# Routing a two-block transformer layer's tokens to 16 experts: selection on logits, facts of the slots in single-pass float32r, idle products in other places, another order of the last rows

## The chip, the cores and the metric

The kernel runs on one core of a Trainium2 chip. The metric is the device time of one execution in microseconds (us); where several executions were timed, their median is given.

## The reference

256 tokens of 1024 features, batch 1, float32, go through two blocks of one layer each. The first block is attention over one key block, retention and a gated feed-forward. The second block has a gated delta rule, a sparse attention over selected keys, a merge of both by two gates, a residual, and then the mixture of experts, which is what this document is about: four groups of four experts; every token takes its best group, in it its two best experts, and weighs them by the probability of the group times the two experts' probabilities, normalized to one. Behind it stands one last normalization of each token.

```python
def hier_moe(h, w_rg, b_rg, w_re, b_re, w1, w3, w2):
    xt = h.reshape(-1, d)                              # h = rmsnorm_2(x, norm2_g)
    glog = (xt @ w_rg + b_rg).astype(jnp.float32)
    gp = jax.nn.softmax(glog, axis=-1)
    gsel = jnp.argmax(glog, axis=-1)
    ggate = jnp.take_along_axis(gp, gsel[:, None], axis=-1)
    elog = (xt @ w_re + b_re).astype(jnp.float32).reshape(-1, N_GROUPS, EXPERTS_PER_GROUP)
    elog_g = jnp.take_along_axis(elog, gsel[:, None, None], axis=1)[:, 0]
    ep = jax.nn.softmax(elog_g, axis=-1)
    top_p, top_i = lax.top_k(ep, TOPK_IN_GROUP)
    top_p = top_p / jnp.sum(top_p, axis=-1, keepdims=True)
    wts = ggate * top_p
    eid = gsel[:, None] * EXPERTS_PER_GROUP + top_i
    comb = jnp.sum(jax.nn.one_hot(eid, N_EXPERTS) * wts[..., None], axis=1)
    act = jax.nn.silu(jnp.einsum("nd,edf->nef", xt, w1)) * jnp.einsum("nd,edf->nef", xt, w3)
    act = act * comb[:, :, None]
    return jnp.einsum("nef,efd->nd", act, w2).reshape(bsz, s, d)
...
        x = x + hier_moe(...)
    return rmsnorm_2(x, final_norm_g)
```

## The kernel before

**Tiles and weights.** Tokens lie in two halves of 128 (`h` is 0 or 1), features in eight blocks of 128 (`m`). All weights come as 134 chunks of 128 x 2048 floats (1 MB), issued on SP's queue by one function (L341; the last four of every 15 chunks of the experts come as two halves of 512 KB into other buffers); the last 48 chunks are the 16 experts'. An expert has three chunks, two for gate and up (`D_EXPERT` is 256) and one for down. Up to the experts every weight is split into a rounded float32r part and a remainder (`whi`, `wlo`, L357 and L358), and each product is done in three single-pass products; the experts' chunks are used as they are, in two passes of float32. For the experts' weights there is room for 15 chunks; each further chunk waits until products have freed a buffer.

**Order.** A scheduler orders each engine's instructions by their dependences and a modelled time. `issue_after(x)` in the code fixes that an instruction comes behind `x` on its engine. `mm` (L374) is the helper of all products, so nearly all of them have that line. `keep_warm(n, ...)` (L1654) issues `n` products of 128 x 128 by 128 x 256 whose result nobody reads: the idle products.

**Routing (`moe_route`, L1698).** The blocks 6 and 7 of the residual `x` come last. Their squares are summed on TensorE, their part of the 20 router logits is added, `rsqrt` gives the normalization, L1716 makes the logits `lg`. `first_max` (L1687) marks the first maximum of four values: a maximum, two comparisons `e`, a maximum `f`, a comparison. It is called for the group (`oh`, L1696). TensorE then transposes the last two pairs of blocks (`turn_t(2)`, `turn_t(3)`, L1665, eight transposes) and makes 14 idle products. On VectorE (DVE) follow `by` (L1727), `eg` (L1729, the four logits of the chosen group's experts), their maximum `em` (L1730), `ex` (L1732, and the exponential on ScalarE (ACT), L1733), `first_max` twice on the exponentials (`oh1`, then `rest`, `oh2`), `sel`, and `oe` (L1741): 16 marks for each token, two of them set. Two products with a triangle of ones (`slt`) and two more for the groups rank the tokens in each expert (`re`) and group (`rg`, both L1751), behind them stand four idle products. `places` (L1758) compares the ranks with 64 slots: `Se` (L1761) says which token lies in which slot of which expert. `turn_s` (L1668) takes each transposed pair of blocks from PSUM: ACT copies it to `xr` (L1673) and rounds it to `thi` (L1674), GpSimd (POOL) makes the remainder `tlo` (L1675); the second call also stores `xr` to DRAM (`xd`, L1677).

**Experts (`moe`, L1766).** 32 products (eight blocks, two halves, `thi` and `tlo`) with `Se[0]` gather the tokens of the first group's four experts into the slots, and ACT and DVE copy them out as `X[0]` and `X[1]` (L1791, L1789). Two experts of 64 slots each make a pair, and there are eight pairs. Beside this the weights of the tokens are made (`dg`, `gs`, `den`, `we`), and `meta` holds 20 numbers of a token: its number, a one, its normalization, its rank in the group, and 16 weights. POOL makes `Sg` (L1823), the slots of the groups. `pc`, four products (L1834 on), counts the tokens of experts and groups. `facts` (L1840) brings `meta` into the slots: 16 products with `Se` (`pair_facts`, `mtp`) and eight with `Sg` (`group_facts`, `mtg`), in two passes each; DVE copies the result (L1849) and makes the row indices (L1851). By these, POOL's gathers fetch the rows of the pairs 2 to 7 from `xd` (`prow`) and the rows of the groups (`grow`).

For the pair `n` come `gate_up` (16 products in two passes each), `act` (silu on ACT, L1913, a product on DVE, L1915), `turn` (two transposes), `down` (eight products; each half of the result is split into `yhi`, L401, on ACT, and `ylo`, L402, on DVE) and `gather` (products of `E` with `yhi` and `ylo` that add both pairs of a group into `y`). In the loop, `pair_facts` and `group_facts` stand behind `gate_up(0)` and ahead of `act(0)`.

**The rows of a group (`finish`, L1962).** For each half of 512 columns: add `y` to the row (L1967, DVE), square and sum (L1968, ACT), multiply by the gain `fng` (L1969, DVE); then the sums are added (`ss`, L1970), `rsqrt` (eight small DVE steps, up to L444), and the row is scaled, 400 columns on ACT (L1972) and 624 on DVE (L1973). A scatter on POOL (L1978) stores it. There are four groups; the last one ends the kernel. A branch behind it (L2022) would recompute everything densely if a slot list had run over.

## Time and profile before

| | before |
|---|---|
| time, median of 3 runs (us) | 779.59 (777.94, 779.61, 779.59) |
| the profiled execution (us) | 776.29, its span 774.1 |
| busy: TensorE (PE), DVE, ACT, POOL (us) | 743.4, 517.4, 357.3, 98.0 |
| mean granted clock of TensorE | 0.979 of full speed |
| moved by DMA | 153.00 MB, mean 198 GB/s |

TensorE is busy 96% of the span, but this share is a mean over stages with different limits. In the forty equal slices of the span (19.4 us each), the moved bytes are mostly under 280 GB/s, and 349 to 417 GB/s in the five slices ahead of the last one, where the experts' weights come; the granted clock is shown with nine tenths or more in all but four of them, one of which (eight tenths) is the slice from 639 to 658 us, that of the routing. In the rows below, a row of the timeline begins with its start and its duration in us, then engine, line, operation, output and inputs, shapes and types, and how many instructions the row joins; in square brackets stands the idle time of the engine ahead of it and what ended it. PEld is the loading of weights into TensorE, SPq the issuing of a DMA. PEclk is the granted clock as a share of full speed, where 1.00 is 2.4 GHz and 0.50 is 1.2 GHz.

### The profile page before, as it was taken

How to read it: one execution, taken by the hardware profiler on the slowest of the kernel's cores; microseconds unless marked ns; L12 is line 12 of the kernel's file. 1: busy time of each engine (PE TensorE's matmuls, PEld its weight loads, DVE VectorE, ACT ScalarE, POOL GpSimd, SP SyncE). 2: the span in 40 equal slices, each digit the busy share in tenths (PEclk: the TensorE clock that was granted, in tenths of full speed). 3: DMA queues.
4: the chain of work that ended last, by engine and by line, in shares of the span. 5: the costliest groups of instructions: out<-in, count | busy, mean ns of one | idle time of the engine just before them, and what ended most of it. 6: DMA issues, size and time to landing. Idle time of an engine off the chain costs nothing. (4 is left out here: it accounts for less than half of the span.)

```text
span 774.1 us, 13914 instructions
## 1 busy us (share of the span) xinstructions
PE 743.4 (96%) x5544; PEld 645.6 (83%) x5544; DVE 517.4 (67%) x1087; ACT 357.3 (46%) x647; POOL 98.0 (13%) x113
## 2 busy tenths in 40 slices
PE   8999999999999999999999989899999999999994
PEld 7998889899999999999989877898889996433421
DVE  6667487777677666788777988876748744333433
ACT  7356444755554454566575424345545522121221
POOL 1000000200000000030010163410001342502100
PEclk9999999999999999999999988999999998999997
DMA  8764333455554555544432341333168793999990
GB/s 308 274 231 160 129 110 120 160 202 173 181 202 163 185 197 171 200 172 166 163 111 82 110 142 51 94 138 110 56 237 360 275 318 135 349 414 417 417 396 27
DMA packets 32949, 153.00 MB, mean 198 GB/s; under 512 B 9712, under 2 KB 10736, under 8 KB 17648
## 3 DMA queue, kind: packets, MB, share of 16 engines
q1 hardware_dynamic: 22464, 141.70, 50.7%
q0 software_dynamic: 2016, 6.29, 2.2%
q10 hardware_dynamic: 8400, 4.08, 1.9%
q8 instruction: 45, 0.74, 0.4%
q14 instruction: 24, 0.20, 0.1%
HBM read 149.57 MB, written 3.54 MB: 198 GB/s over the span
## 5 line engine op out<-in xcount | busy, mean ns | idle before, releaser
L358 DVE TENSOR_TENSOR wlo<-raw,whi 128x1024 fp32r<-128x1024 f32 (+1 forms) x173 | 213.2, 1237 | 82.3 <-ACT whi L357 80.7
L357 ACT ACTIVATE whi<-raw 128x1024 fp32r<-128x1024 f32 (+1 forms) x173 | 180.2, 1045 | 154.2 <-PE acc L374 77.0
L374 PE MATMUL acc<-hhi,wlo 128*128 128x256 f32 x344 | 99.3, 289 | 2.2 <-DVE wlo L358 2.2
L374 PE MATMUL acc<-hhi,whi 128*128 128x256 f32 x344 | 100.4, 292 | 0.0
L374 PE MATMUL sm<-hhi,whi 128*128 128x256 f32 x352 | 99.5, 283 | 0.0
L374 PE MATMUL sm<-hlo,whi 128*128 128x256 f32 x352 | 99.3, 282 | 0.0
L374 PE MATMUL sm<-hhi,wlo 128*128 128x256 f32 x352 | 99.0, 281 | 0.0
L374 PE MATMUL acc<-hlo,whi 128*128 128x256 f32 x344 | 98.9, 288 | 0.0
L374 PEld LDWEIGHTS acc<-hhi,wlo 128*128 128x128 f32 x344 | 66.0, 192 | 3.9 <-DVE wlo L358 2.4
L374 PEld LDWEIGHTS acc<-hhi,whi 128*128 128x128 f32 x344 | 66.3, 193 | 1.4 <-issue 0.8
L374 PEld LDWEIGHTS acc<-hlo,whi 128*128 128x128 f32 x344 | 66.0, 192 | 0.8 <-issue 0.3
L374 PEld LDWEIGHTS sm<-hhi,wlo 128*128 128x128 f32 x352 | 66.6, 189 | 0.0
L374 PEld LDWEIGHTS sm<-hlo,whi 128*128 128x128 f32 x352 | 66.3, 188 | 0.0
L374 PEld LDWEIGHTS sm<-hhi,whi 128*128 128x128 f32 x352 | 66.0, 188 | 0.0
L374 PE MATMUL sm<-raw,X 128*64 128x512 f32 x256 | 61.2, 607 | 0.0
L463 POOL TENSOR_TENSOR sqacc<-sqacc,sq 128x256 f32<-128x256 f32 x19 | 16.2, 852 | 335.2 <-ACT sq L462 334.5
L374 PE MATMUL acc<-alo,whi 128*128 128x256 f32 x176 | 49.5, 281 | 0.0
L374 PE MATMUL acc<-ahi,wlo 128*128 128x256 f32 x176 | 49.4, 281 | 0.0
L374 PE MATMUL acc<-ahi,whi 128*128 128x256 f32 x176 | 49.3, 281 | 0.0
L374 PEld LDWEIGHTS sm<-raw,X 128*64 128x64 f32 x256 | 18.2, 139 | 35.3 <-issue 34.2
L374 PE MATMUL acc<-xhi,wlo 128*128 128x256 f32 x160 | 45.7, 286 | 1.3 <-DVE wlo L358 1.3
L374 PE MATMUL acc<-xhi,whi 128*128 128x256 f32 x160 | 46.0, 288 | 0.9 <-ACT whi L357 0.9
(472 smaller groups left out, 1670.1 us busy)
## 6 DMA issues: line engine op xcount, KB each, us to landing
raw<-in_W_dram SPq DMA_DIRECT2D x119, 1024.0 KB, 5.0
raw<-in_W_dram SPq DMA_DIRECT2D x27, 512.0 KB, 12.1
raw<-in_W_dram SPq DMA_DIRECT2D x4, 256.0 KB, 5.0
xd<-xr ACTq DMA_DIRECT2D x2, 512.0 KB, 2.7
dec<-in_con_dram ACTq DMA_DIRECT2D x2, 384.0 KB
conm<-in_con_dram SPq DMA_DIRECT2D x1, 576.0 KB, 7.1
xa<-in_xT_dram SPq DMA_DIRECT2D x2, 256.0 KB, 4.8
xb<-in_xT_dram SPq DMA_DIRECT2D x2, 256.0 KB
```

Of the source, the lines that this page charges most:

```text
L357: nc.scalar.activation(h, r, AF.Copy)
L358: nc.vector.tensor_tensor(l, r, h.bitcast(F32), ALU.subtract)
L374: return self.nc.tensor.matmul(out, a, b, start=start, stop=stop, **kw).ins
L463: (eng or nc.gpsimd).tensor_tensor(acc, acc, sq, ALU.add)
```

## The change

- **Selection.** `first_max` runs on the logits `eg` themselves, and `rest` subtracts a large number at the first mark. `ex` is gone; the exponential of `eg - em` is made in `moe`, times `sel`, summed into `den`.
- **`tlo`.** DVE makes the remainders of the last two pairs of blocks in place of POOL: two 128 x 256 subtractions behind `oe`, two behind the first two `Se`. The first two pairs stay on POOL.
- **Idle products.** In place of 14 behind the transposes and four behind the ranking: three ahead of the last router products, two ahead of each group of four transposes, nine behind, five behind the ranking.
- **Counts.** `pc` is fixed behind the gather's last product.
- **Facts.** `meta` is split into two float32r parts (`mhl`, 40 columns: rounded part and remainder), so each of the 24 products is one pass of 40 columns. ACT copies the remainders' sums out of PSUM and DVE adds the others. `Sg` becomes float32r.
- **Rows.** In `finish`, the two additions come behind the last `ylo` (`F.split`), the first half's product with `fng` behind both additions, and the second half's product with `fng` joins its scaling in one step. ACT scales the first 512 columns, DVE the last 512.

```diff
@@ turn_s
-    def turn_s(self, m2, tp):
+    def turn_s(self, m2, tp, after=None):
...
-            nc.gpsimd.tensor_tensor(lo, x, hi.bitcast(F32), ALU.subtract)
+            with self.tc.issue_after(after) if after else contextlib.nullcontext():
+                (nc.vector if after else nc.gpsimd).tensor_tensor(lo, x, hi.bitcast(F32), ALU.subtract)
@@ moe_route
         with self.tc.issue_after(done):
+            self.keep_warm(3, self.slt[:, 0], self.thi[0][:, 0:256])
             for m in (6, 7):
...
-            tp = [self.turn_t(2), self.turn_t(3)]
-            self.keep_warm(14, self.slt[:, 0], self.thi[0][:, 0:256])
+            tp = []
+            for m2 in (2, 3):
+                self.keep_warm(2, self.slt[:, 0], self.thi[0][:, 0:256])
+                tp.append(self.turn_t(m2))
+            self.keep_warm(9, self.slt[:, 0], self.thi[0][:, 0:256])
...
-        nc.vector.tensor_reduce(em[:, :, 0], eg, axis=AX.X, op=ALU.max)
-        ex = self.ex = self.t("c", (2, 4), name="ex")
-        nc.vector.tensor_tensor(ex, eg, em.to_broadcast([128, 2, 4]), ALU.subtract)
-        nc.scalar.activation(ex, ex, AF.Exp)
...
-        self.first_max(oh1, ex, self.m1)
-        nc.vector.scalar_tensor_tensor(rest, oh1, -2.0, ex, op0=ALU.mult, op1=ALU.add)
-        self.first_max(oh2, rest, self.m2)
+        self.first_max(oh1, eg, em)
+        nc.vector.scalar_tensor_tensor(rest, oh1, -BIG, eg, op0=ALU.mult, op1=ALU.add)
+        self.first_max(oh2, rest, self.t("c", (2, 1), name="m2"))
...
+        self.turn_s(2, tp[0], chosen)
...
-            self.keep_warm(4, self.slt[:, 0], self.thi[0][:, 0:256])
+            self.keep_warm(5, self.slt[:, 0], self.thi[0][:, 0:256])
...
         self.places(0)
-        for i in range(2):
-            self.turn_s(2 + i, tp[i])
+        self.turn_s(3, tp[1], self.placed)
@@ moe
+        we = c3("we")
+        nc.vector.tensor_tensor(we, self.eg, b4(self.em), ALU.subtract)
+        nc.scalar.activation(we, we, AF.Exp)
+        nc.vector.tensor_tensor(we, we, self.sel, ALU.mult)
         den = c3("den", 1)
-        nc.vector.tensor_tensor(den, self.m1, self.m2, ALU.add)
+        nc.vector.tensor_reduce(den[:, :, 0], we, axis=AX.X, op=ALU.add)
...
-        we = c3("we")
-        nc.vector.tensor_tensor(we, self.sel, self.ex, ALU.mult)
...
+        mhl = self.t("t1", (2, 40), F32R, name="mhl")
+        nc.vector.tensor_copy(mhl[:, :, 0:20], meta[:, :, 0:20])
+        nc.vector.tensor_tensor(mhl[:, :, 20:40], meta[:, :, 0:20], mhl[:, :, 0:20].bitcast(F32), ALU.subtract)
...
-                    mm(pm[:, i], s[h].bitcast(F32), meta[:, h, 0:20], i == 0 and h == 0, h == 1, skip_group_check=True)
+                    mm(pm[:, i], s[h], mhl[:, h], i == 0 and h == 0, h == 1, skip_group_check=True)
...
-            nc.vector.tensor_copy(mt, pm)
+            nc.scalar.activation(mt, pm[:, :, 20:40], AF.Copy)
+            nc.vector.tensor_tensor(mt, pm[:, :, 0:20], mt, ALU.add)
@@ finish
             for n, o in enumerate(halves):
-                nc.vector.tensor_tensor(o, y[n], o, ALU.add)
+                with self.tc.issue_after(F.split) if F.split else contextlib.nullcontext():
+                    nc.vector.tensor_tensor(o, y[n], o, ALU.add)
                 nc.scalar.activation(y[n], o, AF.Square, accum_out=ss[:, n:n + 1])
-                nc.vector.tensor_tensor(o, o, fng[:, 512 * n:512 * n + 512], ALU.mult)
+            nc.vector.tensor_tensor(halves[0], halves[0], fng[:, 0:512], ALU.mult)
...
-            nc.scalar.activation(row[:, 624:], row[:, 624:], AF.Copy, scale=rr)
-            nc.vector.tensor_scalar(row[:, 0:624], row[:, 0:624], rr, None, op0=ALU.mult)
+            nc.scalar.activation(halves[0], halves[0], AF.Copy, scale=rr)
+            nc.vector.scalar_tensor_tensor(halves[1], halves[1], rr, fng[:, 512:1024], op0=ALU.mult, op1=ALU.mult)
```

The order of TensorE at the routing, as a piece of the difference (`thi,slt` are the idle products, L1665 the transposes, `ms` the router's weights):

```order
 L374 MATMUL sm<-ones,sq 128x1 x4
+L374 MATMUL acc<-thi,slt 128x256 x3
 L374 MATMUL sm<-ms,x_7206 128x20 x4
-L1665 MATMUL acc<-con,x_7206 128x128 x8
-L374 MATMUL acc<-thi,slt 128x256 x14
+L374 MATMUL acc<-thi,slt 128x256 x2
+L1665 MATMUL acc<-con,x_7206 128x128 x4
+L374 MATMUL acc<-thi,slt 128x256 x2
+L1665 MATMUL acc<-con,x_7206 128x128 x4
+L374 MATMUL acc<-thi,slt 128x256 x9
 L374 MATMUL sm<-oe,slt 128x32
```

The idle products, 14 in a row before, now stand ahead of, between and behind the transposes, with three more ahead of the last router products.

DVE at the end of the routing, in the changed kernel:

```order
+L1743 TENSOR_TENSOR oe<-sel,oh 128x32
+L1677 TENSOR_TENSOR tlo<-xr,thi 128x256 x2
+L1754 SCALAR_TENSOR_TENSOR re<-sm,oe 128x32
+L1754 SCALAR_TENSOR_TENSOR rg<-sm,oh 128x8
+L1763 TENSOR_TENSOR Se<-con,re 128x256 x2
+L1677 TENSOR_TENSOR tlo<-xr,thi 128x256 x2
+L1798 TENSOR_TENSOR dg<-ms,gm 128x8
```

Before, `oe`, `re`, `rg`, the two `Se` and `dg` followed each other directly; two pairs of `tlo` have moved in between.

DVE at the end of the kernel, as a piece of the difference (the rows of the last group, whose last `ylo` is the fourth of the row `x4`):

```order
-L1967 TENSOR_TENSOR row<-acc,row 128x512
-L402 TENSOR_TENSOR ylo<-acc,yhi 128x512
-L1969 TENSOR_TENSOR row<-row,fng 128x512
-L1967 TENSOR_TENSOR row<-acc,row 128x512
-L1969 TENSOR_TENSOR row<-row,fng 128x512
-L1970 TENSOR_TENSOR ss<-ss 128x1
+L1984 SCALAR_TENSOR_TENSOR row<-row,ry,fng 128x512
+L1925 SCALAR_TENSOR_TENSOR ea__8436<-sm,rc,sl 128x256
+L402 TENSOR_TENSOR ylo<-acc,yhi 128x512 x4
+L1978 TENSOR_TENSOR row<-acc,row 128x512 x2
+L1980 TENSOR_TENSOR row<-row,fng 128x512
+L1981 TENSOR_TENSOR ss<-ss 128x1
```

The last `ylo` now stands ahead of both additions, and one product with `fng` is gone from between them and the sum.

## Rows read from the trace of the kernel before

**Rows 1.** Stretches: length; busy (count) PE, PEld, DVE, ACT, POOL; PEclk, DMA, GB/s

```profile
640.00:652.00 12.00, 12.00 (x62) 9.52 (x64) 6.73 (x33) 4.32 (x11) 4.66 (x8) 0.72 0.15 45
...
663.00:670.00 7.00, 7.00 (x33) 2.01 (x30) 1.79 (x12) 0.38 (x1) 5.96 (x7) 0.95 0.79 215
670.00:752.00 82.00, 80.78 (x380) 30.63 (x382) 32.16 (x73) 18.84 (x41) 12.14 (x15) 1.00 1.02 417
```

**Rows 2.** Timeline, the weights' issues on SP, 650 to 672 us

```profile
651.90 4.24 SPq L341 DMA_DIRECT2D raw<-in_W_dram  x4
...
666.02 4.80 SPq L341 DMA_DIRECT2D raw<-in_W_dram  x4
```

**Rows 3.** Waits, 750 to 760 us (total, times, longest), and timeline of TensorE

```profile
PEld acc L374 <- DMA raw<-in_W_dram: 0.3, 1, 0.3
...
757.63 3.65 PE L374 MATMUL acc<-raw,at 128*64 128x512 f32 x14
```

**Rows 4.** Timeline of DVE and POOL at the routing

```profile
635.06 2.79 POOL L1675 TENSOR_TENSOR tlo<-xr,thi 128x256 fp32r<-128x256 f32 x4 [4.01 <-ACT thi L1674]
...
635.18 0.66 DVE L1727 TENSOR_TENSOR by<-ms,oh 128x32 f32<-128x32 f32 x1
...
636.09 0.16 DVE L1730 TENSOR_REDUCE em<-eg 128x2 f32<-128x8 f32 x1
...
636.77 0.16 DVE L1690 TENSOR_REDUCE m<-ex 128x2 f32<-128x8 f32 x1 [0.28 <-ACT ex L1733]
636.97 0.90 DVE L1693 SCALAR_TENSOR_TENSOR e<-ex,m,con 128x4 f32<-128x4 f32 x2
...
638.70 0.36 DVE L1693 SCALAR_TENSOR_TENSOR e<-rest,m,con 128x4 f32<-128x4 f32 x2
...
639.68 0.19 DVE L1741 TENSOR_TENSOR oe<-sel,oh 128x32 fp32r<-128x32 f32 x1
...
641.21 0.76 DVE L1761 TENSOR_TENSOR Se<-con,re 128x256 fp32r<-128x256 f32 x2
```

**Rows 5.** Timeline of TensorE: transposes, ranking, gathering products

```profile
632.91 1.92 PE L1665 MATMUL acc<-con,x 128*128 128x128 f32 x8
...
639.93 0.59 PE L374 MATMUL sm<-oe,slt 128*128 128x32 f32 x2 [2.70 <-DVE oe L1741]
...
641.80 0.53 PE L374 MATMUL acc<-Se,thi 128*128 128x256 f32 x1
...
646.61 0.28 PE L374 MATMUL acc<-Se,thi 128*128 128x256 f32 x1
...
647.67 0.28 PE L374 MATMUL acc<-Se,tlo 128*128 128x256 f32 x1
```

**Rows 6.** Stretches of the routing, for the granted clock (eighth figure)

```profile
632.95:636.35 3.40, 3.40 (x19) 3.40 (x19) 3.16 (x20) 2.12 (x7) 1.29 (x2) 0.50 0.67 239
636.40:639.70 3.30, 0.83 (x7) 0.63 (x6) 2.68 (x14) 0.52 (x2) 1.45 (x3) 1.00 0.80 318
639.80:646.50 6.70, 6.57 (x30) 6.54 (x31) 4.85 (x25) 2.80 (x6) 1.35 (x3) 0.50 0.22 63
```

**Rows 7.** Timeline of the last rows: DVE, TensorE and ACT

```profile
762.59 0.68 DVE L402 TENSOR_TENSOR ylo<-acc,yhi 128x512 fp32r<-128x512 f32 x1
...
763.32 0.50 PE L374 MATMUL acc<-ylo,E 128*128 128x512 f32 x1 [0.86 <-DVE ylo L402]
...
764.12 0.68 DVE L1967 TENSOR_TENSOR row<-acc,row 128x512 f32<-128x512 f32 x1
...
765.65 0.69 DVE L1969 TENSOR_TENSOR row<-row,fng 128x512 f32<-128x512 f32 x1 [0.85 <-ACT acc L1968]
...
767.91 0.63 ACT L1972 ACTIVATE row<-row,ry 128x400 f32<-128x400 f32 x1 [2.30 <-DVE ry L444]
```

**Rows 8.** Timeline of TensorE, the products of `facts` (two passes each)

```profile
655.24 3.75 PE L374 MATMUL acc<-ms,Se 128*128 128x20 f32 x32
658.84 2.29 PE L374 MATMUL acc<-ms,Sg 128*128 128x20 f32 x16
```

More of the change, by code (lines that the diff above doesn't have):

```diff
@@ L1797, in moe @@
         nc.scalar.activation(dg, dg, AF.Exp)
-        warm = self.t("c", name="warm")[:, 0:1]
-        nc.scalar.activation(warm, dg[:, 0, 0:1], AF.Silu)
         gs = c3("gs", 1)
@@ L1817, in moe @@
             self.places(g)
-        Sg = [self.t("t1", (2, 128), name="Sg") for _ in range(4)]
+        Sg = [self.t("t1", (2, 128), F32R, name="Sg") for _ in range(4)]
         place = c3("gplace")
@@ L1828, in moe @@
         pc = self.ps("sm", (20,))
[L1829 to L1832 removed]
+        with self.tc.issue_after(done):
+            for h in range(2):
+                mm(pc[:, 0:4], self.slt[:, 1], self.oh[:, h], h == 0, h == 1, skip_group_check=True)
+            for h in range(2):
+                mm(pc[:, 4:20], self.slt[:, 1], self.oe[:, h], False, h == 1, skip_group_check=True)
         cn = self.t("c", name="cn")[:, 0:2]
@@ L2021, in moe @@
         reg = nc.values_load(ci[0:1, 0:1], min_val=0, max_val=2 * S)
+        F.split = None
         with self.tc.If(reg > 128):
```

25 lines of the change are left out of this document (11 added, 14 removed).

## The prediction, made before the changed kernel ran

> **What bounds the kernel now.** I read the stretches of the profile first, for the clock and the transfers, then the chain of the routing in the timeline, then the last 20 us. The weights of the experts come in 48 chunks of 1 MB; 15 of them fit before the first expert is computed. So from 640 to 652 us the transfers stand almost still (45 GB/s), from 652 they run, and from 670 to 752 they run at 417 GB/s with the engines' share at 1.02 [rows 1]. SP can issue the next chunks only when the first expert products have freed buffers: at 651.90, and then at 666.02 [rows 2]. Between the two lies a hole: from 663 to 670 only 215 GB/s move [rows 1]. At the far end the last expert's second products wait for a weight transfer and start at 757.63 [rows 3]; nothing after that is a load. So the end of the kernel is the first freeing of a buffer, plus a stream of transfers with one hole in it, plus the tail behind the last chunk. TensorE is busy all the time from 652 to 752, but it arrives at the last weights a little before they do: a TensorE gain that doesn't also move the stream forward buys nothing.
>
> The first freeing hangs on the routing. There VectorE is the chain: `by`, `eg`, `em`, an exponential on ScalarE, and two selections up to `oe` at 639.68, which TensorE has waited for [rows 4, 5]. The granted clock is 0.50 of full speed (1.2 of 2.4 GHz) from 639.8 to 646.5, after an idle time of 2.70 us on TensorE, so most of the 32 gathering products run at half speed [rows 5, 6].
>
> **The change part by part.** The sum is made against the profiled execution (span 774.10, time 776.29). The three timed runs have their median at 779.59, 3.3 above; I carry the difference over unchanged.
>
> *Selection on logits.* `em` starts at 636.09 and the maximum of the exponentials at 636.77 [rows 4]. The changed chain needs the first only: 0.68 us less. The exponential and its normalization move behind the gather, beside the first expert's products, where DVE and ACT have several us of cover.
>
> *`tlo` from POOL to DVE.* While POOL makes the four `tlo` from 635.06 for 2.79 us, `by` takes 0.66 on DVE where `oe`, of the same size, takes 0.19, and the pair of `e` takes 0.90 where the next pair takes 0.36 [rows 4]. With POOL silent that is 0.47 + 0.54 = 1.01 us. The price: two subtractions of 128x256 stand between `oe` and `re` on DVE, two more behind `Se`. `ylo`, twice as wide, takes 0.68 [rows 7], so two cost between 0.68 and 1.36; I take 0.8. DVE would wait for TensorE's four ranking products there anyway, some 0.7 us at full clock, so 0.1 of it shows (0.6 at the upper bound). `oe` is thus early by 0.68 + 1.01 = 1.69 us.
>
> *Idle products.* 14 + 4 become 3 + 2 + 2 + 9 + 5, with transposes between them. The three ahead of the last router products delay these by 3 x 0.12 = 0.35; the DVE chain reads them about 1 us later, so I cost them at nothing (0.35 if that cover were gone). If the clock holds: from `oe`'s first product at 639.93 to the gather at 641.80 took 1.87 us, four ranking and four idle products at the low clock [rows 5]. At full clock it is 0.8 of `tlo`, then `re`, `rg` and the first `Se` (0.41, half of the row of two and a bit [rows 4]), 1.45 in all: 0.42 gained. The gather's 32 products took from 641.80 to about 647.79: until 646.61 at the low clock, 0.213 apart, then ten more at 0.118 [rows 5]. All at 0.118 are 3.78: 2.21 gained. ScalarE now puts a second small exponential between the first and the second of its eight `X`, which has to wait for DVE; I take 0.1 off. The first freeing comes early by 1.69 + 0.42 + 2.21 - 0.1 = **4.2 us**, between 1.6 (clock down as before) and 4.3.
>
> *The slots' facts.* Now 48 products of fp32 (24 of two passes), 655.24 to 661.13, 0.1125 us apart [rows 8]. Single-pass, there are 24: 2.7 us at the same spacing, so TensorE is through 3.1 us sooner; if it fell to the low clock right there, 24 x 0.21 = 5.1 and only 0.7. What is added: two DVE steps (`mhl`), done long before behind the `X`, and per set a copy on ACT ahead of the DVE sum instead of one DVE copy, some 0.35 us longer for the row indices; but the change also lets the indices of the pairs go ahead of the groups' facts, so POOL's row gathers start no later against TensorE. The first activation now stands behind both ACT copies; the first transposes may wait about 0.1. What this buys is the hole: seven us at 215 of 417 GB/s lose 7 x (1 - 215/417) = 3.4 us of transfers [rows 1]. With TensorE 3.1 sooner the chunks of 666.02 are issued about when the queue runs dry. I take the smaller, less the 0.1: **3.0 us**; bounds 0.7 and 3.4.
>
> *The last rows.* Before, DVE adds the first half of the rows ahead of the last `ylo`, which starts at 762.59 though its input was ready some 0.6 sooner; then the first `fng` product delays the second addition, and the second `fng` product (765.65, 0.69) stands right ahead of the sum `ss`, which needs only the second square's read-out [rows 7]. The changed order puts both `ylo` first (0.61), takes `fng` from between (0.24; the second addition started at 764.12, TensorE's last product ended at 763.82) and lets `ss` follow the read-out (the 0.69, of which I count 0.60, since DVE also overlaps the start of a row with the end of the one before): 1.45. The last scaling becomes 512 columns on each engine: ACT took 0.63 for 400 [rows 7], so 0.6 to 0.8, and DVE's two-tensor form 0.7; 0.1 back. Gain **1.35 us**. On the first three groups of rows the same order costs nothing: they lie under the stream.
>
> Sum: 4.2 + 3.0 + 1.35 = 8.55. 776.29 - 8.55 = 767.7 for the profiled execution, 779.59 - 8.55 = **771.0** on the scale of the median.
>
> A rule speaks against the idle products. The stretch of 632.95 to 636.35 runs at 0.50; TensorE is busy in it without a gap, at first with eight transposes, then with idle products, and behind it the clock is up again [rows 5, 6]. So work of this kind raised it here. The Trainium skill ("TensorE: Matmul & The Clock Gate", Part 4: PE-mode transpose) says that transposes don't count as busy time for the clock. By that rule the products set around the transposes would have to hold the clock alone, and it would fall as in the first rival below; the trace cannot separate the two, since both kinds stand in the one stretch.
>
> **The rivals.**
>
> *The clock falls again.* The last idle products end about 635.6 and the ranking starts at 638.2: 2.6 us without work, as long as the 2.70 after which the clock was down before [rows 5]. For it: that length. Against: more dense work on both sides, and it depends on where the gap lies against the chip's own looking. If the low clock covers ranking, idle products and a quarter of the gather, the 4.2 becomes 3.0; if it covers two thirds as before, 1.6. Times: 772.2 to 773.6; I name 772.8.
>
> *The hole is not closed by the facts.* If the stream's end is set elsewhere (the scattered rows that share the queues' last us, or the row gathers), TensorE's 3.0 us turn into waiting at the last chunks: 779.59 - 5.55 = 774.0. For it: the last chunk shares the engines with a scatter. Against: before that the stream runs 82 us at full rate [rows 1], so bytes moved earlier must end earlier.
>
> *More than forecast.* The timed runs lie 3.3 above the profiled one; if that is more time at the low clock in the routing and the facts, the change can return part of it: 10 to 11 us, 769.
>
> *Slower.* The clock falls in the gap before `oe` and stays down through gather, first expert and facts. Price, at twice the spacing: gather 32 x 0.095 = 3.0, first expert (16 pairs; the last expert's 7 pairs take 3.65 with the last one's drain [rows 3], some 0.43 each) 6.9, facts 2.5: 12.4, so 783.4. It decides from the point where the gather alone doesn't raise the clock. Against: it did before, after some 5 us of gathering [rows 5, 6].
>
> *It doesn't do what it says:* if the scheduler had kept the old order nothing would move; but the order of the changed program shows the idle products, the `tlo` and the last rows where they are meant to be.
>
> **How the numbers follow.** Forecast 0.55; clock falls again 0.23; hole not closed 0.12, some of it together with a falling clock (776); more than forecast 0.07; slower 0.02; the remaining 0.01 for no change. The range has to reach from the bigger gain to the hole that stays, with the bounds of the facts (0.7) and of the clock (1.6): 768.6 to 774.6. About 0.3% (2.3 us) is what a measurement of this kernel can tell from no change. Faster by more than that: everything but the slower case, the null case and a thin edge of two rivals at once: 0.94; within: 0.04; slower: 0.02.
>
> **What would show it.** In the profile of the changed kernel: `oe` about 1.7 us sooner, with `by` near 0.2 and both pairs of `e` near 0.36; the granted clock at 1.00 through the gather and its products 0.12 apart; the first freeing of a buffer (SP's issue of 651.90) near 647.7; the facts in about 2.7 us; no stretch near 215 GB/s within 15 us of that issue; the last expert's weight wait some 7 us sooner; `ss` right behind the second read-out. I am wrong if the issue comes early but the weight wait at the end doesn't follow, if the gather's products lie 0.21 apart, or if DVE reaches `re` more than 0.6 us after TensorE's ranking.

## The result and the profile after

The changed kernel took 769.64 us (median of 4 runs, 768.37 to 771.76) beside 779.6 us of the kernel before (777.94 to 782.64): a ratio of 0.9892 with the interval 0.9867 to 0.9918, or 8.4 us of gain (6.4 to 10.4); the two medians themselves lie 10.0 us apart. In a second group of runs the ratio was 0.9891 (0.9873 to 0.9910). The forecast was 8.55 us of gain, 771.0 us. The profiled execution of the changed kernel took 770.57 us, its span 768.4; that of the kernel before took 776.29.

Two executions don't reach the routing at the same time, since the 630 us ahead of it vary by a microsecond or two (in the two rows below by 1.88 us). So everything below is counted from one event, the last addition to the residual on DVE, in front of the router. Its row in the timeline (start, duration), first in the kernel before, then in the changed one:

```profile
629.93 0.75 DVE L1476 SCALAR_TENSOR_TENSOR x<-acc,x 128x256 f32<-128x256 f32 x2 [6.29 <-PE acc L374]
```

```profile
631.81 0.76 DVE L1476 SCALAR_TENSOR_TENSOR x<-acc,x 128x256 f32<-128x256 f32 x2 [6.29 <-PE acc L374]
```

The second profile of the changed kernel is that of `after_again`, below. The freeing of a buffer is read from SP's next issue of a chunk of weights; these issues come in pairs.

| us from there to | before | changed | changed, second profile |
|---|---|---|---|
| `oe` | 9.75 | 8.08 | 8.83 |
| the gather's first product | 11.87 | 9.76 | 10.52 |
| the first freeing of a buffer | 21.97 | 17.72 | 18.48 |
| the third pair of issues | 36.09 | 29.22 | 28.29 |
| the last expert's second products | 127.70 | 121.41 | 122.14 |
| the end of the span | 144.2 | 136.6 | 137.4 |

**Routing.** The timeline of DVE and of TensorE in the changed kernel, the answer to [rows 4, 5], and a stretch for [rows 6] (columns as in [rows 1]):

```profile
637.05 0.21 DVE L1733 TENSOR_TENSOR by<-ms,oh 128x32 f32<-128x32 f32 x1
...
637.30 2.08 PE L374 MATMUL acc<-thi,slt 128*128 128x256 f32 x9
...
637.72 0.36 DVE L1695 SCALAR_TENSOR_TENSOR e<-eg,em,con 128x4 f32<-128x4 f32 x2
...
639.89 0.19 DVE L1743 TENSOR_TENSOR oe<-sel,oh 128x32 fp32r<-128x32 f32 x1
640.00 0.75 DVE L1677 TENSOR_TENSOR tlo<-xr,thi 128x256 fp32r<-128x256 f32 x2
...
640.13 0.39 PE L374 MATMUL sm<-oe,slt 128*128 128x32 f32 x2 [0.75 <-DVE oe L1743]
...
640.78 0.19 DVE L1754 SCALAR_TENSOR_TENSOR re<-sm,oe 128x32 f32<-128x32 f32 x1
...
641.57 0.35 PE L374 MATMUL acc<-Se,thi 128*128 128x256 f32 x1
...
645.30 0.28 PE L374 MATMUL acc<-Se,tlo 128*128 128x256 f32 x1
```

```profile
635.61:639.02 3.41, 3.41 (x19) 3.41 (x17) 2.99 (x19) 2.54 (x8) 0.00 (x0) 0.50 0.53 210
```

`by` takes 0.21 where it took 0.66, and the first pair of `e` 0.36 where it took 0.90. The two `tlo` between `oe` and `re` take 0.75 and end as TensorE's ranking does. TensorE has waited 0.75 us for `oe` and not 2.70. The gather runs from 641.57 to 645.30, 3.73 us at 0.12 a product, where it took 5.87 (from the start of its first product to that of its last). The clock isn't at 1.00 all along: it is at 0.50 from 635.61 to 639.02, over the transposes and most of the nine idle products, and at 1.00 from there until behind the facts.

**Facts and stream.** TensorE in the changed kernel, the answer to [rows 8]; then SP's issues for [rows 2]; then stretches for [rows 1] (columns as there):

```profile
652.87 1.96 PE L374 MATMUL acc<-mhl,Se 128*128 128x40 f32 x16
654.68 1.05 PE L374 MATMUL acc<-mhl,Sg 128*128 128x40 f32 x8
655.66 5.35 PE L374 MATMUL sm<-raw,X 128*64 128x512 f32 x16
```

```profile
649.53 0.81 SPq L341 DMA_DIRECT2D raw<-in_W_dram  x2
...
661.03 12.32 SPq L341 DMA_DIRECT2D raw<-in_W_dram  x7
```

```profile
657.00:659.00 2.00, 2.00 (x8) 0.73 (x6) 1.88 (x12) 0.00 (x0) 1.69 (x2) 0.50 1.00 422
...
661.00:663.00 2.00, 2.00 (x11) 0.76 (x12) 0.00 (x0) 0.38 (x1) 1.65 (x3) 1.00 1.01 373
663.00:665.00 2.00, 2.00 (x11) 0.54 (x8) 0.00 (x0) 0.00 (x0) 1.52 (x3) 1.00 0.98 315
665.00:667.00 2.00, 2.00 (x14) 1.23 (x16) 1.38 (x3) 0.48 (x1) 1.78 (x3) 1.00 1.00 387
...
670.00:745.00 75.00, 74.86 (x348) 27.76 (x344) 28.30 (x65) 16.88 (x38) 9.55 (x11) 1.00 1.02 417
```

The facts take 2.79 us, 652.87 to 655.66, where they took 5.82. The hole is nearly gone: the three stretches from 661 to 667 lose 2 x (3 - (373 + 315 + 387)/417) = 0.84 us of transfers, where 3.4 were lost before. Behind the facts, though, the clock is at 0.50 again (656.09 to 659.50), and the 16 products from 655.66 take 5.28 us up to the next instruction at 660.94, where 16 such products at full clock take about 3.6.

**The end.** The last expert's second products start at 753.22, behind an idle time of TensorE:

```profile
753.22 3.65 PE L374 MATMUL acc<-raw,at 128*64 128x512 f32 x14 [0.55 <-SPq L2034]
```

The row names an event of SP's queue as what ended the wait, not a transfer. The packets of the trace tell more: the last one of the weights ends at 752.71, 0.51 us ahead of these products, and before it ended at 757.12, also 0.51 ahead of 757.63. So in both kernels these products wait for their weights. In the last stretch ahead of them, transfers are few:

```profile
751.00:753.00 2.00, 1.67 (x4) 0.38 (x3) 0.41 (x1) 0.00 (x0) 0.00 (x0) 1.00 0.11 45
```

The last rows, the answer to [rows 7]:

```profile
757.54 0.69 DVE L402 TENSOR_TENSOR ylo<-acc,yhi 128x512 fp32r<-128x512 f32 x1 [1.03 <-ACT yhi L401]
...
758.14 1.37 DVE L1978 TENSOR_TENSOR row<-acc,row 128x512 f32<-128x512 f32 x2
...
759.66 0.69 DVE L1980 TENSOR_TENSOR row<-row,fng 128x512 f32<-128x512 f32 x1
...
760.14 0.19 ACT L1979 ACTIVATION_READ_ACCUMULATOR acc<-row 128x1 f32 x1
760.36 0.16 DVE L1981 TENSOR_TENSOR ss<-ss 128x1 f32<-128x1 f32 x1
```

Both additions follow the last `ylo`, and `ss` follows the second read-out. From 753.22 to the end of the span are 15.2 us, where 16.5 were.

### The profile page after: what moved, and what is told of

It is laid out like the page before. It is cut to its first block, busy times and chain, and to the rows that moved or that the text cites. A ratio compares the mean times of both kernels' runs of the same rounds, so it can differ in the third digit from the quotient of the medians.

```text
span 768.4 us, 13868 instructions
## 1 busy us (share of the span) xinstructions
PE 739.2 (96%) x5523; PEld 639.7 (83%) x5523; DVE 517.1 (67%) x1088; ACT 358.3 (47%) x649; POOL 95.6 (12%) x109
## 3 DMA queue, kind: packets, MB, share of 16 engines
q0 software_dynamic: 2016, 6.29, 2.1%
```

## The experiments

The stages were open in four places: whether the facts really move the stream, what holds the clock at the ranking, what POOL and the exponential cost, and what ends the stream. Each kernel is the changed one with one edit (`k3_split_skip` has two), except `o_warm`, which is the kernel before with one. The runs were timed in several groups, each beside the kernel before; kernels of different groups are compared by their ratios to it.

**The changed kernel again (`after_again`).**

> The changed kernel again, as the control of this group and to narrow its ratio. By the working of the prediction its gain is 8.55 us, a ratio of 0.989. By the trace of the changed kernel, counted from the last addition to the residual (the last two 128x256 additions ahead of the router, 629.93 us before and 631.81 us after), the last expert's second products start 6.3 us sooner and the rest is 1.3 us shorter: 7.6 us, a ratio of 0.990. A ratio under 0.987 would mean that the stages ahead of the routing run faster too.

Measured: 769.04 us, a ratio of 0.9891 (0.9873 to 0.9910). Two stretches of its trace (columns as in [rows 1]):

```profile
631.35:638.17 6.82, 6.82 (x33) 6.79 (x33) 5.36 (x37) 2.53 (x8) 0.00 (x0) 0.50 0.51 184
...
651.00:660.00 9.00, 9.00 (x56) 4.81 (x56) 3.89 (x24) 1.29 (x4) 4.35 (x5) 1.00 1.00 416
```

The same program meets the low clock in other places. Here it begins 1.7 us earlier than in the first profile, counted from the last addition, at the router's logits, and lasts 6.82 us instead of 3.41, so that the marks come 0.75 us later; but behind the facts (651 to 660) it doesn't fall at all, and the third pair of issues is 0.9 us sooner. At the end of the span the two executions differ by 0.7 us.

**Facts in two passes again (`u_facts`).**

```diff
-                    mm(pm[:, i], s[h], mhl[:, h], i == 0 and h == 0, h == 1, skip_group_check=True)
+                    mm(pm[:, i], s[h].bitcast(F32), meta[:, h, 0:20], i == 0 and h == 0, h == 1, skip_group_check=True)
...
-            nc.scalar.activation(mt, pm[:, :, 20:40], AF.Copy)
-            nc.vector.tensor_tensor(mt, pm[:, :, 0:20], mt, ALU.add)
+            nc.vector.tensor_copy(mt, pm)
```

> The changed kernel with the facts of the slots in two-pass fp32 as before (20 columns, one copy on DVE). Theory: the first freeing of a buffer stays where it is (17.7 us after the last addition to the residual); the facts take 5.8 us in place of 2.8; the transfers fall below full rate for some 7 us again (3.3 us of transfers lost, 0.84 in the changed kernel); the last expert's second products start 2.0 to 2.5 us later, so the time is 2.0 to 2.5 us over the changed kernel's. Rival (the end of the stream is set elsewhere, so that the facts buy nothing): the hole is back, but the last second products start within 0.5 us of the changed kernel's place.

Measured: 772.62 us, 0.9933 (0.9912 to 0.9953), so 0.0042 or 3.3 us over the changed kernel in the same group. The first freeing is where it was (17.60 us). Two stretches:

```profile
652.82:663.06 10.24, 10.24 (x38) 6.76 (x39) 3.79 (x24) 0.47 (x1) 3.11 (x4) 0.50 0.69 273
...
660.00:662.00 2.00, 2.00 (x8) 0.62 (x6) 1.85 (x12) 0.00 (x0) 1.65 (x3) 0.50 0.28 51
```

The hole is back, down to 51 GB/s, and the end of the span comes 141.5 us after the last addition, 4.8 and 4.1 later than in the two profiles of the changed kernel. The rival falls: the facts do move the end. In this execution they cost more than the 2 to 2.5 us expected: the clock stayed low for 10.24 us from the middle of the facts through the second pair's first products, and the facts alone took 8.0 us, where they took 5.8 in the trace of before. The timed 3.3 us have an interval of some 2.2 us either way and don't tell this from 2 to 2.5. Nor is it the hole alone that moved the end here: the last weights land 125.32 us after the last addition (120.90 and 121.64 in the changed kernel), but the last second products follow 0.92 us behind them and not 0.51, so TensorE was later still, by 0.4 us.

**Idle products in the old places (`u_warm`), and only they in the new places (`o_warm`).**

```diff
-            self.keep_warm(3, self.slt[:, 0], self.thi[0][:, 0:256])
...
-            tp = []
-            for m2 in (2, 3):
-                self.keep_warm(2, self.slt[:, 0], self.thi[0][:, 0:256])
-                tp.append(self.turn_t(m2))
-            self.keep_warm(9, self.slt[:, 0], self.thi[0][:, 0:256])
+            tp = [self.turn_t(2), self.turn_t(3)]
+            self.keep_warm(14, self.slt[:, 0], self.thi[0][:, 0:256])
...
-            self.keep_warm(5, self.slt[:, 0], self.thi[0][:, 0:256])
+            self.keep_warm(4, self.slt[:, 0], self.thi[0][:, 0:256])
```

> The changed kernel with the idle products where they were before: none ahead of the last router products, 14 behind all eight transposes, 4 behind the ranking. Theory (the places of the idle products hold the clock): it falls to 0.50 at the ranking, the gather's products lie 0.21 us apart for at least half of the gather, and the first freeing of a buffer comes 1.5 to 3 us later than in the changed kernel, the end as much. Rival (it is the shorter wait of TensorE ahead of the ranking, which selection on logits and the remainders on DVE bring, that holds the clock): the products lie 0.12 us apart as in the changed kernel and the time is the same within 0.5 us.

> The kernel before with only the idle products changed: 3 ahead of the last router products, 2 ahead of each four transposes, 9 behind them, 5 behind the ranking. Theory (the length of TensorE's wait ahead of the ranking decides, not the places): the wait stays above 2 us, since the selection still ends 9.75 us after the last addition to the residual; the clock falls to 0.50 at the ranking, the gather's products lie 0.21 us apart for more than half of it, the first freeing stays at about 22 us after that addition, and the time is within 1 us of before. Rival (the places hold the clock): the gather's products lie 0.12 us apart, the first freeing comes 2.2 to 2.6 us sooner and the time is 2 to 2.6 us lower.

Measured: `u_warm` 769.69 us, 0.9898 (0.9883 to 0.9914), within 0.7 us of the changed kernel in the same group; `o_warm` 779.39 us, 1.0006 (0.9986 to 1.0026) to before. TensorE and a stretch in `u_warm`, then the same in `o_warm`:

```profile
636.18 3.33 PE L374 MATMUL acc<-thi,slt 128*128 128x256 f32 x14
639.32 0.55 PE L374 MATMUL sm<-oe,slt 128*128 128x32 f32 x2
```

```profile
633.16:639.98 6.82, 6.82 (x34) 6.78 (x34) 6.10 (x38) 2.42 (x8) 0.00 (x0) 0.50 0.72 262
```

```profile
643.91 0.59 PE L374 MATMUL sm<-oe,slt 128*128 128x32 f32 x2 [3.06 <-DVE oe L1745]
```

```profile
643.74:650.57 6.83, 6.66 (x31) 6.66 (x32) 4.97 (x25) 2.80 (x6) 1.36 (x3) 0.50 0.21 64
```

In `u_warm` the clock is at 0.50 from 633.16 to 639.98, so the 14 products run slowly enough to reach up to the ranking without a wait; behind it the clock is at 1.00, and the gather takes 3.59 us, with the idle products in their old places. In `o_warm` they stand in the new places, TensorE waits 3.06 us, the clock is at 0.50 again from 643.74 on and the gather takes 5.70 us. So the places of the idle products are worth nothing that these runs can tell. What goes with the clock in the gather is how long TensorE waits ahead of the ranking. DVE sets the end of this wait; its start hangs on the clock itself, since slow idle products fill it. A kernel without idle products was not run.

**Transposes in place of the idle products (`t_turns`).**

```diff
     def keep_warm(self, n, a, b):
 
+        if hasattr(self, "slt"):
+            p = self.ps("acc", (128,))
+            for _ in range(n):
+                self.nc.tensor.transpose(p, self.x[4][:, 0:128], self.con("ident"))
+            return
```

> The changed kernel with each idle product of the routing replaced by one more 128x128 transpose whose result nobody reads, at the same places and in the same numbers. It tells apart what the trace before could not: whether transposes raise or hold the granted clock as the idle products do. If they do, the clock is at 1.00 at the ranking and in the gather, the gather's products lie 0.12 us apart, and the time is the changed kernel's. If they don't count, the clock is at 0.50 at the ranking and through most of the gather, its products lie 0.21 us apart, the first freeing of a buffer comes 2 to 3 us later, and so does the end. The Trainium skill (TensorE: Matmul & The Clock Gate, Part 4: PE-mode transpose) says the latter.

Measured: 769.53 us, 0.9899 (0.9881 to 0.9916), the changed kernel's time within 0.6 us. A stretch of its trace and three rows of TensorE (L1659 and L1670 are transposes):

```profile
632.13:635.53 3.40, 3.40 (x18) 3.40 (x18) 3.12 (x22) 1.34 (x5) 0.00 (x0) 0.50 0.62 229
```

```profile
634.36 1.06 PE L1670 MATMUL acc<-con,x 128*128 128x128 f32 x4
635.21 1.30 PE L1659 MATMUL acc<-con,x 128*128 128x128 f32 x9
637.44 0.39 PE L374 MATMUL sm<-oe,slt 128*128 128x32 f32 x2 [0.93 <-DVE oe L1748]
```

From 632.62 up to the ranking TensorE runs nothing but transposes, the clock is at 0.50 at first, and behind that stretch the nine transposes from 635.21 are at full speed (about 0.14 us each where those of 634.36 are 0.21); the gather takes 3.59 us. So these transposes raise the clock and hold it as products do. The Trainium skill (TensorE: Matmul & The Clock Gate, Part 4: PE-mode transpose) says of the transpose mode that it doesn't count as busy time in the same way; for the float32 transposes of this kernel the measurement speaks against it.

**Remainders on POOL again (`u_pool`), and selection on exponentials again (`u_sel`).**

```diff
-        self.turn_s(2, tp[0], chosen)
...
-        self.turn_s(3, tp[1], self.placed)
+        for i in range(2):
+            self.turn_s(2 + i, tp[i])
```

```diff
-        self.first_max(oh1, eg, em)
-        nc.vector.scalar_tensor_tensor(rest, oh1, -BIG, eg, op0=ALU.mult, op1=ALU.add)
-        self.first_max(oh2, rest, self.t("c", (2, 1), name="m2"))
+        nc.vector.tensor_reduce(em[:, :, 0], eg, axis=AX.X, op=ALU.max)
+        ex = self.ex = self.t("c", (2, 4), name="ex")
+        nc.vector.tensor_tensor(ex, eg, em.to_broadcast([128, 2, 4]), ALU.subtract)
+        nc.scalar.activation(ex, ex, AF.Exp)
...
+        self.first_max(oh1, ex, self.m1)
+        nc.vector.scalar_tensor_tensor(rest, oh1, -2.0, ex, op0=ALU.mult, op1=ALU.add)
+        self.first_max(oh2, rest, self.m2)
```

> The changed kernel with the last four remainders on POOL again, as before. Theory (DVE is slowed while POOL works): the marks of the chosen group's logits take 0.66 us in place of 0.21, one comparison 0.7 in place of 0.22, and the selection ends 1.0 us later, 9.1 us after the last addition to the residual; DVE then goes to the ranks 0.1 to 0.3 sooner. TensorE's wait ahead of the ranking grows from 0.75 to some 1.8 us. With the clock held the first freeing is 0.7 to 1.0 us later; with the clock fallen 2.5 to 3.5. Rival (POOL has nothing to do with it): both take 0.2 as in the changed kernel and nothing moves.

> The changed kernel with the experts selected on the exponentials again. Theory: the marks of the experts come 0.65 to 0.75 us later (from 2.83 us behind the start of the product with the group's marks to 3.5), TensorE's wait ahead of the ranking grows as much, to about 1.4 us at most; with the clock held the first freeing and the end are 0.6 to 0.8 us later; with the clock fallen, as with the remainders on POOL, 2.5 to 4 us later. Rival: the exponential hides in a wait that is there anyway: no change.

Measured: `u_pool` 773.03 us, 0.9926 (0.9900 to 0.9952); `u_sel` 772.38 us, 0.9922 (0.9897 to 0.9947): by the ratios 2.7 and 2.4 us over the changed kernel. Neither was timed in one group with it, and these differences have intervals of some 2.5 us either way, so that they only just stand out. POOL, DVE and TensorE in `u_pool`:

```profile
637.67 2.81 POOL L1677 TENSOR_TENSOR tlo<-xr,thi 128x256 fp32r<-128x256 f32 x4 [5.76 <-ACT thi L1675]
637.82 0.61 DVE L1698 TENSOR_TENSOR oh<-e,f 128x8 f32<-128x8 f32 x1
...
638.46 0.66 DVE L1739 SCALAR_TENSOR_TENSOR rest<-oh,eg 128x8 f32<-128x8 f32 x1
...
639.35 1.14 DVE L1695 SCALAR_TENSOR_TENSOR e<-rest,m,con 128x4 f32<-128x4 f32 x2
...
641.36 0.39 PE L374 MATMUL sm<-oe,slt 128*128 128x32 f32 x2 [1.57 <-DVE oe L1743]
```

While POOL subtracts, three of DVE's small steps take 0.61, 0.66 and 1.14 us where they take 0.17, 0.17 and 0.36 else: 1.71 us, more than the 1.0 expected, and on other steps than before, since POOL now starts behind `by`. The reductions between them (0.16) are not slowed. TensorE waits 1.57 us, the clock is at 0.50 in the gather from 643.42 to 646.84, and the first freeing comes after 21.50 us, 3.8 and 3.0 later than in the changed kernel's two profiles.

ACT, DVE and TensorE in `u_sel`, and a stretch:

```profile
637.59 0.21 ACT L1741 ACTIVATE ex<-ex 128x8 f32<-128x8 f32 x1
...
637.84 0.16 DVE L1692 TENSOR_REDUCE m<-ex 128x2 f32<-128x8 f32 x1 [1.60 <-ACT ex L1741]
...
640.45 0.59 PE L374 MATMUL sm<-oe,slt 128*128 128x32 f32 x2 [1.82 <-DVE oe L1748]
```

```profile
632.87:646.50 13.63, 11.81 (x55) 11.52 (x55) 10.60 (x60) 3.89 (x13) 0.00 (x0) 0.50 0.41 140
```

Here the exponential costs 1.6 us of waiting, not 0.28 as in [rows 4]: it stands behind ACT's copies of the transposed blocks. TensorE waits 1.82 us, and the clock, at 0.50 since the router's logits, doesn't come back before 646.53, near the end of the gather; the first freeing comes after 22.2 us. So in these profiles neither edit alone has the gather at full clock; the shorter wait needs both.

**What ends the stream: fewer scatters (`no_scatter`), TensorE sooner (`k1_facts_split`).**

```diff
@@ no_scatter, in store of scatter(g): the rows of the first three groups are not stored
+                if g < 3:
+                    return
@@ k1_facts_split
             def amid():
+                if n == 0:
+                    pair_facts()
+                if n == 1:
+                    group_facts()
+                    grow[0] = rows(F.idg[:, 0, 0:1])
...
-                pair_facts()
...
-                group_facts()
...
```

> The changed kernel without the scatters of the first three groups' rows: 1.57 MB less on the queues beside the weights (3.8 us of transfers at 417 GB/s), and these three groups' rows are not stored; all else is as in the changed kernel. It tells what ends the stretch from 670 us on. If the stream of transfers alone sets the last expert's start, that start and the end come some 3.5 us sooner. If TensorE arrives almost together with the last weights (it waits there for 0.5 to 0.9 us in the changed kernel's trace), the gain is no more than that wait, 0.5 to 1 us, and the last products then follow those ahead of them without a wait for weights.

> The changed kernel with the facts in two places: the 16 products of the pairs in the middle of the first pair's gate and up products, the 8 of the groups in the middle of the second pair's, in place of all 24 in a row between them; the first gathers of rows on POOL follow the pairs' facts, that of the first group's rows the groups' facts. Theory: the stretch at 0.50 that follows the facts in one profile of the changed kernel (24.3 to 27.7 us after the last addition to the residual) comes from the 24 small products in a row; split, the clock stays at 1.00, the third freeing of buffers comes 26.5 to 27 us after the last addition (29.2 and 28.3 in the two profiles of the changed kernel), and since TensorE and the stream end close together, the last expert's second products start 0.5 to 1.5 us sooner: a time 0.5 to 1.5 us under the changed kernel's. Rival: the weights alone set the end, and the second freeing, 1.8 us later than in the changed kernel, opens a hole of its own: the same time or up to 1 us more.

Measured: `no_scatter` 767.2 us, 0.9856 (0.9820 to 0.9893); `k1_facts_split` 770.72 us, 0.9902 (0.9871 to 0.9934), no gain over the changed kernel that the runs can tell. The software queue (packets, MB, share) of `no_scatter` on its page, and its last products' row:

```profile
q0 software_dynamic: 1584, 5.47, 1.8%
```

```profile
750.60 3.65 PE L374 MATMUL acc<-raw,at 128*64 128x512 f32 x14
```

The scatters skip empty slots, so only 6.29 - 5.47 = 0.82 MB went away and not the 1.57 of the expectation: 2.0 us at 417 GB/s. The end came 135.5 us after the last addition, 1.8 sooner than in `after_again` and 1.1 sooner than in the first profile. The last weights land after 117.55 us, 3.4 and 4.1 sooner than in the changed kernel's two profiles, so by more than the 2.0 us of bytes; why is open. The last products stand 2.48 us behind them instead of 0.51: here they wait for TensorE's own work. In `k1_facts_split` the clock stayed at 1.00 behind the facts and the third pair of issues came after 26.5 us, 1.8 to 2.7 sooner than in the changed kernel's two profiles. Yet its end came after 136.4 us, only 0.2 and 0.9 sooner, and there its last products still wait for weights (0.50 us behind the last packet); in between a small hole had opened:

```profile
751.18 3.65 PE L374 MATMUL acc<-raw,at 128*64 128x512 f32 x14 [0.30 <-SPq L2037]
```

```profile
654.00:656.00 2.00, 2.00 (x12) 0.71 (x9) 0.54 (x2) 0.44 (x1) 1.30 (x2) 1.00 0.89 258
```

So bytes taken from the queues bring the end forward, up to TensorE's own limit 1.4 to 2.1 us ahead (the last products after 120.03 us, in the changed kernel after 121.41 and 122.14); TensorE's products made sooner bring little or nothing by themselves. The stream of transfers ends last in the changed kernel.

**Fewer bytes: gathers that skip the empty slots (`k2_skip`), and the same with the split facts (`k3_split_skip`).**

```diff
-            nc.vector.tensor_copy(idx[:, 0], mt[:, :, 0])
+            idf = self.t("c", name="idf")[:, 0:n]
+            nc.vector.tensor_scalar(idf, mt[:, :, 1], -1000.0, 1000.0, op0=ALU.mult, op1=ALU.add)
+            nc.vector.tensor_tensor(idx[:, 0], idf, mt[:, :, 0], ALU.add)
...
```

> The changed kernel in which the gathers of rows skip the empty slots: their row index is put out of bounds, as that of the scatters is already, so these rows are not fetched and nobody needs what stands there. 1280 rows of 4 KB are fetched now for the experts' pairs 2 to 7 and the four groups; the scatters of all groups move 256 (software queue: 6.29 MB in all). About half of the fetched rows go away, some 2.5 MB, 6 us of transfers at 417 GB/s. Theory (the stream of transfers ends last, with TensorE close behind): the last expert's second products start without a wait for weights, and the time is 1 to 2.5 us under the changed kernel's, TensorE being the limit from there on (without 0.82 MB of scatters the end came 1.85 us sooner). Rival: a skipped row costs its queue as much as a fetched one, or the weights don't profit: the same time.

> Both of it: the facts in two places (as in k1_facts_split) and the gathers without the empty slots (as in k2_skip). Theory: k1_facts_split gave TensorE a lead that the stream took back; with 2.5 MB less on the stream the lead counts, so the time is 1 to 2 us under that of k2_skip alone where that has a stretch at 0.50 behind the facts, and 2 to 4 us under the changed kernel's. Rival: TensorE's own sequence of products is the limit in both, and the two differ by less than 0.5 us.

Measured: `k2_skip` 767.17 us, 0.9860 (0.9833 to 0.9887), the fastest of the kernels that store every row, by the ratios about 2.4 us under the changed kernel; the two were not timed in one group, and their intervals overlap at the edge. `k3_split_skip` 768.24 us, 0.9865 (0.9841 to 0.9889), the same. The software queue of `k2_skip`, two late stretches and its last products' row:

```profile
q0 software_dynamic: 2016, 3.52, 1.2%
```

```profile
735.00:745.00 10.00, 8.86 (x44) 2.95 (x42) 3.57 (x13) 2.47 (x7) 1.71 (x2) 1.00 0.66 271
745.00:755.00 10.00, 9.59 (x32) 2.89 (x28) 3.45 (x6) 2.39 (x5) 0.00 (x0) 1.00 0.02 9
```

```profile
749.31 3.65 PE L374 MATMUL acc<-raw,at 128*64 128x512 f32 x14
```

2.77 MB less (6.6 us at 417 GB/s) move the end only 2.3 us, counted from the last addition (137.4 in `after_again`, 135.0 here): the last weights land after 115.85 us, 3.95 us ahead of the last products, and TensorE is the limit. Why the split facts bring nothing then is only in part clear: in this profile of `k2_skip` the clock didn't fall behind the facts either, so there was nothing to save there; that `k3_split_skip` ends 0.7 us later stays open.

**The last rows in the old order (`u_tail`).**

```diff
-                with self.tc.issue_after(F.split) if F.split else contextlib.nullcontext():
-                    nc.vector.tensor_tensor(o, y[n], o, ALU.add)
+                nc.vector.tensor_tensor(o, y[n], o, ALU.add)
                 nc.scalar.activation(y[n], o, AF.Square, accum_out=ss[:, n:n + 1])
-            nc.vector.tensor_tensor(halves[0], halves[0], fng[:, 0:512], ALU.mult)
+                nc.vector.tensor_tensor(o, o, fng[:, 512 * n:512 * n + 512], ALU.mult)
...
-            nc.vector.scalar_tensor_tensor(halves[1], halves[1], rr, fng[:, 512:1024], op0=ALU.mult, op1=ALU.mult)
+            nc.vector.tensor_scalar(row[:, 0:624], row[:, 0:624], rr, None, op0=ALU.mult)
```

> The changed kernel with the last rows in the order of before. From the last expert's second products (the row of 14 products of 64 partitions) to the end of the span it took 16.47 us before and 15.18 in the changed kernel; theory: 16.4 to 16.6 here, and what stands ahead is as in the changed kernel; the time is 1.3 us over the changed kernel's. Rival: the first three groups' rows delay something under the stream too, and the last products start later as well.

Measured: 772.33 us, 0.9932 (0.9905 to 0.9959). In its trace (span 768.5):

```profile
751.81 3.65 PE L374 MATMUL acc<-raw,at 128*64 128x512 f32 x14
```

From 751.81 to the end of the span are 16.7 us, 1.5 more than in the changed kernel. The last products stand 120.8 us after the last addition, not later than in the changed kernel (121.4), so the first three groups' rows cost nothing there. The timed 3.2 us over the changed kernel have an interval of some 2.5 us either way and can't confirm the size; the one trace does.

## Why the prediction was right

**The bound** was read rightly: first freeing, stream, tail. `u_facts` put the hole back and moved the end; `no_scatter` and `k1_facts_split` showed from both sides that the stream is what ends last. One line didn't show what the forecast read in it: the wait of 0.3 us for a weight in [rows 3] is that of the products at 751.24, not of those at 757.63. That the latter wait for weights too is shown by the last packet, 0.51 us ahead of them.

**The first freeing**: 4.2 us forecast, 4.25 measured in the first profile and 3.49 in the second. In the first, `oe` came 1.67 sooner (1.69 forecast), from `oe` to the gather took 1.68 in place of 2.12 (0.44; 0.42 forecast), and the gather 3.73 in place of 5.87 (2.14; 2.21 forecast). The covers held too: the remainders on DVE ended with the ranking, and the three idle products ahead of the router didn't show, `by` standing 5.25 us after the last addition before and 5.24 in the changed kernel.

**The cause of the clock**, on which 2.6 of the 4.2 us hang, was left open in the forecast and given to the wrong edit in the weighing. The first rival put 2.6 us without work ahead of the ranking. It was 0.75, since the idle products ran mostly at the low clock and ended at 639.38, and since `oe` was early; the first of these two was not foreseen, so that this rival failed in part by luck. The new places of the idle products were not needed (`u_warm`), nor enough (`o_warm`). In this study's profiles TensorE's wait ahead of the ranking was 0 to 0.93 us wherever the gather ran at full clock, and 1.57 to 3.06 us where it ran at the low one in part or whole (2.70 before). Two edits that lengthen the wait in different ways (`u_pool`, `u_sel`) lost the full clock, and three that only touch the idle products changed nothing; but `u_sel` shows the clock not coming back, and `before` and `o_warm` show it falling again behind a stretch at 1.00, so that the length of the wait alone decides is argued from these profiles, one for each kernel, and not shown by itself. The rule against transposes, which the forecast let stand as a support of that rival, doesn't hold for this kernel's transposes (`t_turns`).

**The terms don't add as the sum has it.** The sum gave the exponential 0.68 us and POOL 1.01. Undone one at a time, they move the first freeing by 4.5 and 3.8 us (3.7 and 3.0 from the second profile). Of this, 2.1 and 2.3 us are `oe` itself, which then comes after 10.22 and 10.33 us, so each costs more by itself than its term; 1.7 and 1.5 us are the gather, 5.41 and 5.25 us with the low clock in it, where it took 3.73, and in `u_sel` 0.65 us the way from `oe` to the gather, at the low clock too. The sum came out right because both edits were made together.

**The facts**: 3.0 us forecast; the way from the first freeing to the last expert's second products was shortened by 105.73 - 103.69 = 2.04 us, in the second profile by 2.07. This is the mis-sized term. TensorE was through 3.03 us sooner, as reckoned, but the hole didn't close: it shrank by 3.4 - 0.84 = about 2.5 us. The low clock behind the facts, which lies over the second pair's products in the first profile (5.28 us for what took 4.86 before, where the clock was low up to 663.67), isn't the reason: the second profile has none there, and 2 x (3 - (334 + 352 + 401)/417) = 0.79 us of transfers are still lost, from 659 to 665. The forecast took no account of what is left of the hole. Another 0.5 us (0.3 in the second profile) went between the last chunk's issue (6.76 us sooner than before) and its landing (6.29 sooner), for which no cause was shown.

**The total.** The profiles show 7.6 and 6.8 us of gain from the last addition on, less than the 8.55 forecast; the timed gain, 8.4 us, has an interval that holds all three. So that the time agrees to a microsecond or so is in part luck: the facts gave 1 us less than their term. What the two-pass facts cost in an execution varies with the clock (`u_facts` shows 10.24 us at 0.50 from their middle on). This is the mechanism of the rival that gave more than the forecast, and may be why the timed gain lies above the two profiles; that was not shown. Taken from one profiled execution to the other (776.29 to 770.57) the gain is 5.7 us, since the changed one reached the last addition 1.88 us later; the forecast of 767.7 for the profiled execution had no term for that.

**The tail**: 1.35 us forecast, 1.3 measured in both profiles (16.5 to 15.2), 1.5 when undone (`u_tail`).

## What to carry to other kernels

Where a wait of TensorE stands ahead of dense work, price a step that shortens this wait by what the clock does behind it too, not by its own length alone: here two edits priced at 0.7 and 1.0 us, undone one at a time, moved the first freeing by 3 to 4.5 us each, 1.5 to 2.3 of it at the low clock, and the timed end by about 2.5, and new places for the products meant to keep the engine busy were worth nothing that the runs can tell. Where a stream of transfers and an engine end close together, ask for each how far the other lies behind: here weights that landed 3.4 to 5.8 us sooner moved the end by 1.1 to 2.3 us, up to the engine's own limit, and an engine made some 2 us faster in the middle moved it by less than 1. A gather by index that fetches rows for empty slots pays for them in the same stream as the weights; put their index out of bounds if nobody reads the rows.

## What the runs showed of the hardware

- Small DVE steps with two tensor inputs took 0.61 to 0.66 us in place of 0.17 to 0.21 while POOL subtracted 128 x 256 tensors (`u_pool`, [rows 4]), though one of them, `ex` before, took only 0.21 there; a reduction beside them still took 0.16.
- The granted clock of the same program fell to 0.50 behind the facts in one execution and not in another (24.3 to 27.7 us after the last addition, and nowhere there in `after_again`).
- With nothing but 128 x 128 float32 transposes on TensorE from 632.62 us, the clock came back from 0.50 to 1.00 at 635.53 (`t_turns`).
- Products that waited for their weights started 0.50 to 0.52 us behind the last packet of these, in all nine profiles in which they waited (0.51 before and changed).
- Rows whose index is out of bounds move no bytes: 1280 fetched and 256 stored rows were 6.29 MB, and with the empty slots skipped 3.52 MB, in as many packets (2016).
